# Instance normalisation in 3D: chunk sums split as two chunks on VectorE and one on ScalarE, and one mask of 27 entries that hands a matmul's result to chunks

## The chip, the cores and the metric

The kernel runs on one core of a Trainium2 chip; the other cores are idle. Times are device microseconds (us) of one execution. Every run is given a state, and only runs in the fast state are compared. HBM is the chip's main memory, SBUF a core's working memory, PSUM the memory that receives TensorE's results; DMA engines move data between HBM and SBUF, and a transfer that is issued can stand in a DMA queue: in the kernel before, a tile's store took 54.2 us from issue to landing, while one tile was stored every 29.0. A tile is a block of 128 partitions x 12288 fp32 values, 6.29 MB. A tile's *landing* is the moment at which its load from HBM is complete, and its *store issue* the moment at which its way back to HBM is ordered.

## The reference

```python
# x: float32 (8, 64, 32, 64, 64), eps: 1e-5
mean = np.mean(x, axis=(2, 3, 4), keepdims=True)
var = np.var(x, axis=(2, 3, 4), keepdims=True)
return (x - mean) / np.sqrt(var + eps)
```

There are 8 x 64 = 512 instances of 131072 values each, 268.4 MB in and 268.4 MB out.

## The kernel before

The tensor is read once and written once. It is cut into two small parts of 128 x 4096 and 42 tiles of 128 x 12288. Four tiles have a place in SBUF at a time, the four *slots*. SyncE issues the loads, ScalarE the stores; a slot is loaded again when its store is complete. One row of a tile holds three *chunks* of 4096, each from one instance; one instance lies in 32 consecutive chunks. So a mean needs three steps: sums of chunks, a sum over 32 chunks that lie on several partitions (a matmul with a block matrix of 1/n), and handing the result back to each chunk. The same is done for the squares.

```python
def over_instance(eng, a, p, at, m, to, negate, c1, wait, steps):   # runs on VectorE
    n = THIRDS                                                      # 3
    ...
    eng.tensor_tensor(out=block(a, by_both, n, m), in0=spread(a, at, m),
                      in1=belongs[:, :, :m], op=Alu.mult)._wait_ge(*wait).then_inc(steps[0], 1)
    # here TensorE multiplies by_both with the block matrix into psum p
    eng.tensor_reduce(out=a[:, by_instance : by_instance + n], in_=p..., axis=AXIS, op=Alu.add)
    eng.tensor_tensor(out=block(a, by_chunk, n, n), in0=spread(a, by_instance, n),
                      in1=belongs[:, :, :n].rearrange("p i c -> p c i"), op=Alu.mult)
    eng.tensor_reduce(out=a[:, to : to + n], in_=block(a, by_chunk, n, n), axis=AXIS,
                      op=Alu.add, negate=negate)                    # waits and increments cut

def tile_on_vector(eng, t, lane, c1, c3, c4, c16):
    ...
    for j, part in ((0, chunk[0]), (3, t[:, COLS - TURN :])):       # 4096, and 1536 of chunk 2
        eng.reduce_sum(out=column(a, SUMS, j), in_=part, axis=AXIS)._wait_ge(
            landed[lane], c16).then_inc(summed[lane], 1)
    over_instance(...)                                              # means
    ...  # chunk 0: subtract the mean, sum of squares
    over_instance(...)                                              # variances
    ...  # 1/root, shifts; chunk 0 and chunk 1 scaled in place

def tile_on_scalar(eng, t, lane, c1, c3, c4, c16, dst):
    ...
    for j, part in ((1, chunk[1]), (2, chunk[2][:, : CHUNK - TURN])):   # 4096, and 2560 of chunk 2
        eng.activation(out=unused..., in_=part, func=Act.Identity,
                       accum_out=column(a, SUMS, j))
    ...  # sums of squares of chunks 1 and 2, root, chunk 2 scaled in place
    eng.dma_start(out=dst, in_=t)._wait_ge(done[lane], c3).then_inc(stored[lane], 16)

def load_all(eng):                                                  # on SyncE
    ...
    with eng.Fori(1, ROUNDS) as it:
        for s in range(SLOTS):
            eng.dma_start(out=slots[s][:], in_=x_t[it * SLOTS + s])._wait_ge(
                stored[s], c16).then_inc(landed[s], 16)
```

The last tile has code of its own (`last_on_vector` and so on), which the change doesn't touch.

## Time and profile before

| | before |
|---|---|
| time, median of 6 runs | 1247.28 us (1247.02 to 1249.46) |
| moved over HBM | 536.9 MB, 431 GB/s over the span |
| busy: VectorE, ScalarE, TensorE | 65%, 61%, 4% |
| pace in the middle | one tile per 29.0 us |
| landing to store issue, a middle tile | 21.9 us |

The shares of the page are averages over the run, and none of them says by itself what sets the end. Two more readings are needed. The first is the page's list of DMA issues (kB each, median us from issue to landing):

```profile
slot<-in_x_dram SPq DMA_DIRECT2D x42, 6144.0 KB, 39.9
out_dram<-slot ACTq DMA_DIRECT2D x41, 6144.0 KB, 54.2
```

The second is one tile in the timeline (start, us, engine, line and operation; in brackets the idle time ahead of it):

```profile
653.89 6.08 DVE L173 TENSOR_REDUCE small<-slot 128x1 f32<-128x4096 f32 x2 [7.03 <-DMA slot<-in_x_dram]
...
660.00 0.17 DVE L141 TENSOR_TENSOR small<-small,belongs 128x12 f32<-128x12 f32 x1
660.23 0.50 PEld L266 LDWEIGHTS psum<-small,avg 128*128 128x128 f32 x2 [19.39 <-DVE small L141]
660.23 0.60 PE L266 MATMUL psum<-small,avg 128*128 128x12 f32 x2 [19.29 <-DVE small L141]
660.86 0.17 DVE L147 TENSOR_REDUCE small<-psum 128x3 f32<-128x12 f32 x1 [0.69 <-PE psum L266]
661.07 0.17 DVE L153 TENSOR_TENSOR small<-small,belongs 128x9 f32<-128x9 f32 x1
661.27 0.16 DVE L159 TENSOR_REDUCE small<-small 128x3 f32<-128x9 f32 x1
...
675.77 0.34 ACTq L256 DMA_DIRECT2D out_dram<-slot  x1
```

The first line is the tile's landing, the last its store issue. The three lines after the matmul (L147, L153, L159) are the hand-out that the change shortens: each starts 0.20 us after the one ahead of it.

### The profile page before, as it was taken

The numbers are of one execution on the slowest core, as the hardware profiler recorded it, in microseconds if no ns is written. First come the engines' busy times: TensorE is split into PE (matmuls) and PEld (weight loads), VectorE is DVE, ScalarE is ACT, GpSimd is POOL, SyncE is SP. The second block draws the span as 40 slices with busy tenths as digits, with TensorE's granted clock in tenths as the row PEclk, the third lists the DMA queues.
The fourth block names the chain that finished last, engine by engine and source line by source line (L and its number), as shares of the span: only waits on it lengthen the run. The fifth ranks groups of instructions, "written<-read, shape, count | busy, mean of one in ns | idle before, by whom it ended". The sixth has DMA issues, their size and how long they took to land.

```text
span 1245.3 us, 1977 instructions
## 1 busy us (share of the span) xinstructions
PE 52.7 (4%) x176; PEld 44.1 (4%) x176; DVE 808.7 (65%) x739; ACT 753.7 (61%) x435; POOL 4.0 (0%) x21
## 2 busy tenths in 40 slices
PE   0000000000000000000000000000000000000000
PEld 0000000000000000000000000000000000000000
DVE  2887666666666666666666666666666666666662
ACT  5876555666566666655556665666566555566661
POOL 1000000000000000000000000000000000000000
DMA  9999999999999999999999999999999999999998
GB/s 396 429 430 433 444 433 433 429 431 437 439 433 431 429 433 440 437 429 433 429 436 440 434 429 431 434 437 439 431 429 431 433 440 439 429 431 429 436 440 366
DMA packets 12818, 536.89 MB, mean 431 GB/s; under 512 B 1424, under 2 KB 1424, under 8 KB 1424
## 3 DMA queue, kind: packets, MB, share of 16 engines
q1 hardware_dynamic: 6336, 268.44, 49.9%
q10 hardware_dynamic: 6480, 268.44, 49.8%
q14 instruction: 2, 0.02, 0.0%
HBM read 268.44 MB, written 268.44 MB: 431 GB/s over the span
## 4 chain that ended last, share of the span: by engine, by line
another core or an unknown queue 82%; DMA 9%; DVE 3%; ACT 2%; SPq 1%; issue 1%; PE 0%; ACTq 0%; DVEq 0%
DMA slot<-in_x_dram 6%; DMA out_dram<-slot 4%; ACT unused L236 1%; SPq L543 1%; DVE stats L332 1%; DVE small L173 0%; ACT unused L229 0%; DVE slot L216 0%; DVE slot L209 0%; ACT slot L422 0%; PE psum L266 0%; DVE slot L372 0%; PE psum L435 0%; SPq L541 0%
## 5 line engine op out<-in xcount | busy, mean ns | idle before, releaser
L229 ACT ACTIVATE unused<-slot 128x4096 uint8<-128x4096 f32 x82 | 243.4, 2968 | 302.9 <-DMA slot<-in_x_dram 300.5
L173 DVE TENSOR_REDUCE small<-slot 128x1 f32<-128x4096 f32 x82 | 249.2, 3081 | 272.8 <-DMA slot<-in_x_dram 272.8
L236 ACT ACTIVATE unused<-slot,small 128x4096 uint8<-128x4096 f32 x82 | 303.4, 3701 | 63.7 <-DVE small L159 63.7
L187 DVE CUSTOM_DVE_ANT_0 unused<-slot 128x4096 uint8<-128x4096 f32 x41 | 181.4, 4426 | 1.4
L249 ACT ACTIVATE slot<-slot,small 128x4096 f32<-128x4096 f32 x41 | 155.9, 3801 | 18.0 <-DVE small L204 18.0
L216 DVE TENSOR_SCALAR slot<-slot,small 128x4096 f32<-128x4096 f32 x41 | 98.7, 2406 | 0.0
L180 DVE TENSOR_SCALAR slot<-slot,small 128x4096 f32<-128x4096 f32 x41 | 96.5, 2353 | 1.5
L266 PE MATMUL psum<-small,avg 128*128 128x9 f32 (+1 forms) x164 | 49.1, 375 | 1116.7 <-DVE small L141 1116.7
L209 DVE TENSOR_SCALAR slot<-slot,small 128x4096 f32<-128x4096 f32 x41 | 96.2, 2346 | 0.0
L266 PEld LDWEIGHTS psum<-small,avg 128*128 128x128 f32 x164 | 41.1, 311 | 1124.7 <-DVE small L141 1124.7
L147 DVE TENSOR_REDUCE small<-psum 128x3 f32<-128x12 f32 x82 | 13.8, 169 | 56.6 <-PE psum L266 56.6
L243 ACT ACTIVATE small<-small,eps_t 128x3 f32<-128x3 f32 x41 | 12.2, 299 | 61.1 <-DVE small L159 61.1
L141 DVE TENSOR_TENSOR small<-small,belongs 128x12 f32<-128x12 f32 x82 | 13.9, 169 | 31.2 <-ACT unused L236 28.8
L201 DVE RECIPROCAL small<-small 128x3 f32<-128x3 f32 x41 | 7.2, 175 | 15.0 <-ACT small L243 15.0
L153 DVE TENSOR_TENSOR small<-small,belongs 128x9 f32<-128x9 f32 x82 | 13.9, 170 | 2.8
L229 ACT ACTIVATION_READ_ACCUMULATOR unused<-slot 128x1 f32 x82 | 15.3, 187 | 0.0
L236 ACT ACTIVATION_READ_ACCUMULATOR unused<-slot,small 128x1 f32 x82 | 15.3, 187 | 0.0
L159 DVE TENSOR_REDUCE small<-small 128x3 f32<-128x9 f32 x82 | 13.3, 162 | 2.8
L332 DVE BATCH_NORM_STATS2 stats<-slot 128x6 f32<-128x512 f32 (+1 forms) x15 | 8.8, 662 | 7.2 <-DMA slot<-in_x_dram 7.2
L448 DVE TENSOR_REDUCE small<-slot 128x1 f32<-128x2048 f32 x2 | 4.6, 2282 | 8.9 <-DMA slot<-in_x_dram 8.9
L390 ACT ACTIVATE unused<-slot 128x4096 uint8<-128x4096 f32 (+1 forms) x2 | 4.4, 2208 | 8.0 <-DMA slot<-in_x_dram 8.0
L474 ACT ACTIVATE unused<-slot,small 128x4096 uint8<-128x4096 f32 x2 | 7.4, 3707 | 2.0 <-DVE small L451 2.0
(50 smaller groups left out, 52.4 us busy)
## 6 DMA issues: line engine op xcount, KB each, us to landing
slot<-in_x_dram SPq DMA_DIRECT2D x42, 6144.0 KB, 39.9
out_dram<-slot ACTq DMA_DIRECT2D x41, 6144.0 KB, 54.2
out_dram<-slot ACTq DMA_DIRECT2D x3, 2048.0 KB, 23.6
slot<-in_x_dram SPq DMA_DIRECT2D x2, 2048.0 KB, 10.0
out_dram<-slot ACTq DMA_DIRECT2D x1, 4096.0 KB, 17.6
```

The source lines that it names most:

```text
L141: eng.tensor_tensor(out=block(a, by_both, n, m), in0=spread(a, at, m), in1=belongs[:, :, :m], op=Alu.mult,)._wait_ge(*wait).then_inc(steps ...
L153: eng.tensor_tensor(out=block(a, by_chunk, n, n), in0=spread(a, by_instance, n), in1=belongs[:, :, :n].rearrange("p i c -> p c i"), op=Alu ...
L173: eng.reduce_sum(out=column(a, SUMS, j), in_=part, axis=AXIS)._wait_ge(landed[lane], c16).then_inc(summed[lane], 1)
L180: eng.tensor_scalar(out=chunk[0], in0=chunk[0], scalar1=column(a, MEANS, 0), scalar2=None, op0=Alu.add,)._wait_ge(centred[lane], c1).then_ ...
L187: eng.tensor_tensor_reduce(out=unused[2][:], in0=chunk[0], in1=chunk[0], scale=1.0, scalar=0.0, op0=Alu.mult, op1=Alu.add, accum_out=colum ...
L209: eng.tensor_scalar(out=chunk[0], in0=chunk[0], scalar1=column(a, SCALES, 0), scalar2=None, op0=Alu.mult,)._wait_ge(scaled[lane], c1).then ...
L216: eng.tensor_scalar(out=chunk[1], in0=chunk[1], scalar1=column(a, SCALES, 1), scalar2=column(a, SHIFTS, 1), op0=Alu.mult, op1=Alu.add,)._w ...
L229: eng.activation(out=unused[j - 1][:, : part.shape[1]], in_=part, func=Act.Identity, accum_out=column(a, SUMS, j),)._wait_ge(landed[lane], ...
L236: eng.activation(out=unused[j - 1][:], in_=chunk[j], func=Act.Square, bias=column(a, MEANS, j), accum_out=column(a, SQUARES, j),)._wait_ge ...
L249: eng.activation(out=chunk[2], in_=chunk[2], func=Act.Identity, scale=column(a, SCALES, 2), bias=column(a, SHIFTS, 2),)._wait_ge(shifted[l ...
L266: eng.matmul(out=p[:, col : col + THIRDS * m], lhsT=avg[PART][:], rhs=a[:, at + m : at + m + THIRDS * m], start=True, stop=True,)._wait_ge ...
L332: i = eng.bn_stats(out=stats[:, g, :], in_=t[:, at : at + size])
```

## The change

Its intent is to have fewer instructions: one reduction on VectorE covers chunks 0 and 1 and gives two columns at once, ScalarE sums chunk 2 whole, and after each matmul one multiplication with a mask of 3 x 9 entries and one reduction take the place of reduce, multiply, reduce.

```diff
-        for j, part in ((0, chunk[0]), (3, t[:, COLS - TURN :])):
-            eng.reduce_sum(out=column(a, SUMS, j), in_=part, axis=AXIS)...
+        eng.reduce_sum(
+            out=a[:, SUMS : SUMS + 2],
+            in_=t[:, : 2 * CHUNK].rearrange("p (c f) -> p c f", f=CHUNK),
+            axis=AXIS,
+        )._wait_ge(landed[lane], c16).then_inc(summed[lane], 1)
 ...
-        for j, part in ((1, chunk[1]), (2, chunk[2][:, : CHUNK - TURN])):
-            eng.activation(out=unused[j - 1]..., in_=part, func=Act.Identity, accum_out=column(a, SUMS, j))
+        eng.activation(out=unused[0][:], in_=chunk[2], func=Act.Identity, accum_out=column(a, SUMS, 2))
 ...
-        eng.tensor_reduce(out=a[:, by_instance : by_instance + n], in_=p..., axis=AXIS, op=Alu.add)
-        eng.tensor_tensor(out=block(a, by_chunk, n, n), in0=spread(a, by_instance, n), in1=belongs..., op=Alu.mult)
+        eng.tensor_tensor(
+            out=block(a, by_chunk, n, n * n),
+            in0=p.unsqueeze(1).to_broadcast([P, n, n * n]),
+            in1=belongs9[:].rearrange("p c i j -> p c (i j)"),
+            op=Alu.mult,
+        )
         eng.tensor_reduce(
             out=a[:, to : to + n],
-            in_=block(a, by_chunk, n, n),
+            in_=block(a, by_chunk, n, n * n),
```

The rest of the diff (cut) is the multiply and the matmul ahead of the hand-out, which shrink from 12 to 9 columns for the means, setup of the mask by three small copies on GpSimd, columns of the scratch tiles, and counts of semaphores.

More of the change, by code (lines that the diff above doesn't have):

```diff
@@ L68 @@
     within = sbuf("within", [P, PART * THIRDS, THIRDS])
-    TURN = 1536
-    belongs = sbuf("belongs", [P, THIRDS, THIRDS + 1])
+    belongs = sbuf("belongs", [P, THIRDS, THIRDS])
+    belongs9 = sbuf("belongs9", [P, THIRDS, THIRDS, THIRDS])
     GROUP = 480
@@ L87 @@
     late = sbuf("late", [P, 96])
-    small = [sbuf(f"small{i}", [P, 72]) for i in range(LANES)]
+    small = [sbuf(f"small{i}", [P, 96 if i < SLOTS else 16]) for i in range(LANES)]
     psum = [
@@ L109 @@
     sorted_ = semaphores("sorted", SLOTS)
-    joined = semaphores("joined", SLOTS)
     picked = semaphores("picked", SLOTS)
@@ L114 @@
     sorted2 = semaphores("sorted2", SLOTS)
-    joined2 = semaphores("joined2", SLOTS)
     picked2 = semaphores("picked2", SLOTS)
     gathered = semaphores("gathered", SLOTS)
-    SUMS, MEANS, SQUARES, VARS, ROOTS, SCALES, SHIFTS = 0, 28, 31, 55, 58, 61, 64
+    SUMS, MEANS, SQUARES, VARS, ROOTS, SCALES, SHIFTS = 0, 39, 42, 81, 84, 87, 90
     AXIS = mybir.AxisListType.X
@@ L129, in block, with over_instance @@
         return a[:, first : first + n * m].rearrange("p (n m) -> p n m", m=m)
-    def spread(a, first, m):
-        return a[:, first : first + m].unsqueeze(1).to_broadcast([P, THIRDS, m])
-    def over_instance(eng, a, p, at, m, to, negate, c1, wait, steps):
+    def over_instance(eng, a, p, at, to, negate, c1, wait, steps):
         n = THIRDS
-        by_both = at + m
-        by_instance = by_both + n * m
-        by_chunk = by_instance + n
+        by_both = at + n
+        by_chunk = by_both + n * n
         eng.tensor_tensor(
-            out=block(a, by_both, n, m),
-            in0=spread(a, at, m),
-            in1=belongs[:, :, :m],
+            out=block(a, by_both, n, n),
+            in0=a[:, at : at + n].unsqueeze(1).to_broadcast([P, n, n]),
+            in1=belongs[:],
             op=Alu.mult,
         )._wait_ge(*wait).then_inc(steps[0], 1)
-        eng.tensor_reduce(
-            out=a[:, by_instance : by_instance + n],
-            in_=p.rearrange("p (n m) -> p n m", m=m),
-            axis=AXIS,
-            op=Alu.add,
-        )._wait_ge(steps[1], c1).then_inc(steps[2], 1)
-        eng.tensor_tensor(
-            out=block(a, by_chunk, n, n),
-            in0=spread(a, by_instance, n),
-            in1=belongs[:, :, :n].rearrange("p i c -> p c i"),
-            op=Alu.mult,
-        )._wait_ge(steps[2], c1).then_inc(steps[3], 1)
+        eng.tensor_tensor(
[3 more added lines that the diff above has]
+            op=Alu.mult,
+        )._wait_ge(steps[1], c1).then_inc(steps[2], 1)
         eng.tensor_reduce(
             out=a[:, to : to + n],
-            in_=block(a, by_chunk, n, n),
+            in_=block(a, by_chunk, n, n * n),
             axis=AXIS,
@@ L164, in over_instance, with tile_on_vector @@
             negate=negate,
-        )._wait_ge(steps[3], c1).then_inc(steps[4], 1)
-    def tile_on_vector(eng, t, lane, c1, c3, c4, c16):
+        )._wait_ge(steps[2], c1).then_inc(steps[3], 1)
+    def tile_on_vector(eng, t, lane, c1, c2, c3, c16):
         a, p = small[lane], psum[lane]
         chunk = [t[:, i * CHUNK : (i + 1) * CHUNK] for i in range(THIRDS)]
-        for j, part in ((0, chunk[0]), (3, t[:, COLS - TURN :])):
-            eng.reduce_sum(out=column(a, SUMS, j), in_=part, axis=AXIS)._wait_ge(
-                landed[lane], c16
-            ).then_inc(summed[lane], 1)
+        eng.reduce_sum(
[3 more added lines that the diff above has]
+        )._wait_ge(landed[lane], c16).then_inc(summed[lane], 1)
         over_instance(
-            eng, a, p[:, 0:12], SUMS, 4, MEANS, True, c1, (summed[lane], c4),
-            (sorted_[lane], meaned[lane], joined[lane], picked[lane], centred[lane]),
+            eng, a, p[:, 0:9], SUMS, MEANS, True, c1, (summed[lane], c2),
+            (sorted_[lane], meaned[lane], picked[lane], centred[lane]),
         )
@@ L197, in tile_on_vector @@
         over_instance(
-            eng, a, p[:, 12:21], SQUARES, 3, VARS, False, c1, (squared[lane], c3),
-            (sorted2[lane], varied[lane], joined2[lane], picked2[lane], gathered[lane]),
+            eng, a, p[:, 9:18], SQUARES, VARS, False, c1, (squared[lane], c3),
+            (sorted2[lane], varied[lane], picked2[lane], gathered[lane]),
         )
@@ L223, in tile_on_vector, with tile_on_scalar @@
         )._wait_ge(shifted[lane], c1).then_inc(done[lane], 1)
-    def tile_on_scalar(eng, t, lane, c1, c3, c4, c16, dst):
+    def tile_on_scalar(eng, t, lane, c1, c2, c3, c16, dst):
         a = small[lane]
         chunk = [t[:, i * CHUNK : (i + 1) * CHUNK] for i in range(THIRDS)]
-        for j, part in ((1, chunk[1]), (2, chunk[2][:, : CHUNK - TURN])):
-            eng.activation(
-                out=unused[j - 1][:, : part.shape[1]],
-                in_=part,
-                func=Act.Identity,
-                accum_out=column(a, SUMS, j),
-            )._wait_ge(landed[lane], c16).then_inc(summed[lane], 1)
+        eng.activation(
+            out=unused[0][:],
+            in_=chunk[2],
+            func=Act.Identity,
+            accum_out=column(a, SUMS, 2),
+        )._wait_ge(landed[lane], c16).then_inc(summed[lane], 1)
         for j in (1, 2):
@@ L258, in tile_on_scalar, with tile_on_tensor @@
         )
-    def tile_on_tensor(eng, t, lane, c1, c3, c4, c16):
+    def tile_on_tensor(eng, t, lane, c1, c2, c3, c16):
         a, p = small[lane], psum[lane]
-        for at, m, col, before, after in (
-            (SUMS, 4, 0, sorted_, meaned),
-            (SQUARES, 3, 12, sorted2, varied),
+        n = THIRDS
+        for at, col, before, after in (
+            (SUMS, 0, sorted_, meaned),
+            (SQUARES, n * n, sorted2, varied),
         ):
             eng.matmul(
-                out=p[:, col : col + THIRDS * m],
+                out=p[:, col : col + n * n],
                 lhsT=avg[PART][:],
-                rhs=a[:, at + m : at + m + THIRDS * m],
+                rhs=a[:, at + n : at + n + n * n],
                 start=True,
@@ L278, with last_on_vector @@
     BOTH2, INST2, CHUNKED2, FOUND, ROOTED, SCALED, SHIFTED = 53, 65, 68, 77, 80, 83, 86
-    def last_on_vector(eng, t, lane, c1, c3, c4, c16):
+    def last_on_vector(eng, t, lane, c1, c2, c3, c16):
         a, p = late, psum[lane]
@@ L383, with last_on_scalar @@
     WEIGHED, WEIGHED2, VARIED, STEPS = 4, 11, 14, 16
-    def last_on_scalar(eng, t, lane, c1, c3, c4, c16, dst):
+    def last_on_scalar(eng, t, lane, c1, c2, c3, c16, dst):
         a = late
@@ L431, in last_on_scalar, with last_on_tensor @@
         ).then_inc(stored[lane], 16)
-    def last_on_tensor(eng, t, lane, c1, c3, c4, c16):
+    def last_on_tensor(eng, t, lane, c1, c2, c3, c16):
         for col, at, ready_at in ((0, BOTH, WEIGHED), (12, BOTH2, WEIGHED2)):
@@ L514, in over_tiles @@
             ctx.enter_context(eng.register(f"{on_tile.__name__}_c{m}"))
-            for m in (1, 3, 4, 16)
+            for m in (1, 2, 3, 16)
         ]
-        for c, m in zip(counts, (1, 3, 4, 16)):
+        for c, m in zip(counts, (1, 2, 3, 16)):
             eng.reg_mov(c, m)
@@ L522, in over_tiles @@
                 on_tile(eng, slots[s][:], s, *counts, *more)
-            for c, m in zip(counts, (1, 3, 4, 16)):
+            for c, m in zip(counts, (1, 2, 3, 16)):
                 eng.reg_add(c, c, m)
@@ L528, in over_tiles @@
             step = on_last if k == n_tiles - 1 else on_tile
-            step(eng, slots[k % SLOTS][:], k % SLOTS, c, 3 * c, 4 * c, 16 * c, *more)
+            step(eng, slots[k % SLOTS][:], k % SLOTS, c, 2 * c, 3 * c, 16 * c, *more)
     def load_all(eng):
@@ L603, in set_up @@
                 eng.tensor_tensor(
-                    out=belongs[:, :, :THIRDS],
-                    in0=within[:, 0:THIRDS, :] if b == 1 else belongs[:, :, :THIRDS],
+                    out=belongs[:],
+                    in0=within[:, 0:THIRDS, :] if b == 1 else belongs[:],
                     in1=within[:, b * THIRDS : (b + 1) * THIRDS, :],
@@ L609, in set_up @@
             )
-        step(
-            eng.tensor_copy(
-                out=belongs[:, :, THIRDS:], in_=belongs[:, :, THIRDS - 1 : THIRDS]
+        for j in range(THIRDS):
+            step(
+                eng.tensor_copy(
+                    out=belongs9[:, :, :, j], in_=belongs[:].rearrange("p i c -> p c i")
+                )
             )
-        )
         for to, c in ((slice(0, THIRDS), slice(0, THIRDS)), (slice(3, 4), slice(1, 2))):
```

## The prediction

> **What bounds the kernel now.** I read the page first (shares of the engines, the DMA row of the 40 slices, the queues), then the windows of one stretch in the middle, then the DMA queues in that same stretch, then who waits for whom. From the page:
>
> ```profile
> PE 52.7 (4%) x176; PEld 44.1 (4%) x176; DVE 808.7 (65%) x739; ACT 753.7 (61%) x435; POOL 4.0 (0%) x21
> DMA  9999999999999999999999999999999999999998
> q1 hardware_dynamic: 6336, 268.44, 49.9%
> q10 hardware_dynamic: 6480, 268.44, 49.8%
> HBM read 268.44 MB, written 268.44 MB: 431 GB/s over the span
> ```
>
> No compute engine is above two thirds, while the DMA row is at its highest digit in every slice but the last. Loads (q1) and stores (q10) each take half of the 16 engines, 99.7% together. The input is read once and the output written once, so the bytes can't shrink. The steady state, four tiles long, in the windows view (columns: stretch, length, busy time of each engine, granted clock, DMA share, GB/s) and then the two queues in that stretch (packets, MB, share):
>
> ```profile
> 600.00:716.00 116.00, 4.79 (x16) 4.00 (x16) 76.52 (x69) 70.49 (x41) 0.00 (x0) 1.00 1.00 434
> ...
> q10 hardware_dynamic: 576, 25.17, 50.1%
> q1 hardware_dynamic: 576, 25.17, 50.1%
> ```
>
> The DMA share is 1.00 and both queues get the same 25.17 MB, four tiles each, in 116.0 us: one tile in and one out per 29.0 us. VectorE works 76.52/4 = 19.1 us of each 29.0, ScalarE 17.6. The waits say the same from the engines' side (engine and line waited for: total us, times, longest):
>
> ```profile
> ACT unused L229 <- DMA slot<-in_x_dram: 300.5, 39, 8.2
> DVE small L173 <- DMA slot<-in_x_dram: 272.8, 39, 7.5
> ...
> SPq L543 <- DMA out_dram<-slot: 1024.5, 36, 28.7
> ```
>
> Both engines wait some 7 to 8 us per tile for a load, and the loading queue waits 28.5 us per tile for a store to free a slot. The last row alone could also be read as a latency loop round the four slots; that is the first rival below.
>
> [...] 434 GB/s at a share of 1.00. So there is nothing to win in the steady state. [...] 576 packets from each queue in the stretch above. So a store that is issued later stands behind what is queued and loses no bandwidth, as long as something is queued. [...] the step from 1536 to 4096 elements costs (4420 - 1742)/2560 = 1.046 ns per element, 0.956 elements per ns. So the reduction over two chunks should gain no speed from its shape.
>
> **The change, part by part.** The rows are those of the groups by form (count, busy us, mean ns):
>
> ```profile
> L173 DVE TENSOR_REDUCE small<-slot 128x1 f32<-128x4096 f32 x41 | 181.2, 4420 | 272.8 <-DMA slot<-in_x_dram 272.8
> L229 ACT ACTIVATE unused<-slot 128x2560 uint8<-128x2560 f32 x41 | 95.1, 2320 | 0.0
> L173 DVE TENSOR_REDUCE small<-slot 128x1 f32<-128x1536 f32 x41 | 71.4, 1742 | 0.0
> L153 DVE TENSOR_TENSOR small<-small,belongs 128x9 f32<-128x9 f32 x82 | 13.9, 170 | 2.8
> L159 DVE TENSOR_REDUCE small<-small 128x3 f32<-128x9 f32 x82 | 13.3, 162 | 2.8
> L147 DVE TENSOR_REDUCE small<-psum 128x3 f32<-128x12 f32 x41 | 7.0, 170 | 28.4 <-PE psum L266 28.4
> ```
>
> (1) The sums on VectorE. Before, 4096 and 1536 elements in two instructions, which the timeline shows as 6.08 us together (they overlap a little, 4420 + 1742 = 6162 ns). After, 8192 elements in one: 4420 + 4096 x 1.046 = 8.70 us. That is +2.62 us on the path from a tile's landing to its store, because the means need it.
> (2) The sums on ScalarE. Before 3617 + 2320 ns plus two reads of an accumulator, done about when VectorE is; after one of 3617 ns plus one read, about 3.8 us. This frees 2.4 us of ScalarE per tile, but takes nothing from the path: VectorE's 8.70 us now end last.
> (3) The hand-out after each of the two matmuls. Before: reduce, multiply, reduce, each starting 0.20 us after the one ahead. After: one multiply over 27 and one reduce over 27. A step is gone (0.20 us); the two that remain have 18 elements more, and I take about 1 ns each from the slope of (1), so +0.02 us each. Saved per hand-out 0.16 us, per tile 0.33 us. That one input of the multiply is in PSUM should not matter: the reduce from PSUM takes 170 ns, as the step of the same kind in SBUF does.
> (4) The multiply ahead of the first matmul has 9 elements instead of 12, and the matmul 9 columns instead of 12: 3 ns and 6 ns by their rows, nothing. The setup on GpSimd gets two more tiny copies, 0.2 us each, while the first load is still on its way (it lands at 8.9 us, setup ended near 6).
>
> Sum per tile: 2.62 - 0.33 = **+2.3 us** from landing to store. A middle tile lands at 653.89 us and its store is issued at 675.77: 21.9 us before, so 24.2 after. VectorE's busy time goes from 19.1 to 19.1 + 8.70 - 6.16 - 0.34 + 0.08 = 21.4 us of 29.0, ScalarE's from 17.6 to about 15.1.
>
> Now what of it reaches the end. In a slot's round, a load takes 39.9 us from issue to landing, the work 21.9 and a store 54.2: 116.0, four times 29.0. But a load and a store need only 29.0 us each at their half of the bandwidth, so 39.9 + 54.2 - 58.0 = 36.1 us per round is standing in a queue. The added 2.3 us comes out of these 36.1, and the pace stays at 29.0. At the start, tile 0 is stored at 52.7 us and the next two follow at 22.2 us, the pace of the engines; they would come at 24.5 us, so the third is stored at 104 instead of 97.2. But then the store queue is still on tile 1's store, which lands at 120.4, so no DMA engine runs dry. At the end, the last tile has its own code, which the change leaves alone (16.4 us from its landing at 1205.96 to its first store at 1222.35). From 1222 us on, 7.57 MB move, of which the last tile is 6.29: 1.28 MB, 3 us of work, is still queued when that store is issued. The store of the tile before goes out 2.3 us later, at 1201, still well inside that queue. So the sum on the time is 0, give or take a microsecond.
>
> **The rivals.** (a) **A latency loop.** If the four slots' round were the bound, each round would grow by 2.3 us, each tile by 2.3/4 = 0.58 us, and 41 tiles by 24 us: 1271 us, 1.9% slower. For it speaks the loading queue's wait of 1024.5 us for stores; against it that the DMA share is 1.00 and 434 GB/s during that wait, which leaves no room. (b) **VectorE becomes the bound.** It would need over 29.0 us per tile; I reckon 21.4. Only if the two-row reduction ran at half speed (8.7 us more) would a tile take 33 us from landing to store; the next tile's sums follow on the same engine, so 41 tiles would need some 1350 us. Nothing in the trace points to it. (c) **The shorter hand-out wins.** 0.33 us per tile off the path, were the path the bound and the sums equal: 3 us at most. It meets the same full DMA. (d) **Start or end.** If the last store found an empty queue because the load of the last tile landed later, some 1 to 3 us are lost; if the later stores let the loads run ahead and the tail stays fuller (its share is 0.89 in 1222 to 1227), about 0.5 us is won.
>
> **Range and chances.** I take the time before, 1247.4 us, unchanged. The three runs before spread from 1247.1 to 1249.5, and (d) adds at most 3 us, so 1244 to 1252 should hold it eight times in ten. Faster by over 2% [...]: 0.01. Slower by over 2% needs a reduction far slower than its slope, or (a) with somewhat more than I reckon: 0.02. Within 2%: 0.97.
>
> **What would show it.** In the profile after: the two-chunk reduction near 8.7 us; the reduce from PSUM gone and a multiply from PSUM of about 0.19 us in its place; landing to store near 24.2 us; VectorE's wait for loads down from 272.8/39 = 7.0 to about 4.7 us per tile, ScalarE's up; load and store latency together shorter by about 2.3 us; stores still spaced by 29.0 us, at 434 GB/s. I would be wrong if the pace were 29.6 us with a DMA share under 1.00 (then (a) holds), if VectorE no longer waited for loads (then (b)), or if the DMA moved fewer GB/s at a full share, for which I have no mechanism.

Four passages are cut from the prediction, at the marks, because no trace or run shows what they said. No term of its sum is among them: +2.3 us per tile is 2.62 - 0.33, from the rows that it quotes, and the sum on the time is 0. Some of its steps rest on less with the cuts. That there is nothing to win in the steady state, and the 0.01 for faster by over 2%, rest on the 434 GB/s at a share of 1.00 alone. That a later store loses no bandwidth was the author's estimate at that time; the runs after it showed it (434 GB/s before and after the change). That the reduction gains no speed from its shape rests on the measured slope of 1.046 ns per element alone.

## The result, and the profile after

| | before | after |
|---|---|---|
| time, median of 6 runs each | 1247.28 us | 1246.41 us (1246.21 to 1248.0) |
| ratio | | 0.9991 (95% interval 0.9978 to 1.0004) |
| VectorE, ScalarE busy | 808.7, 753.7 us | 904.6, 658.6 us |
| load, work, store of a slot's round | 39.9 + 21.9 + 54.2 us | 39.9 + 24.2 + 51.9 us |
| pace | 29.0 us | 29.0 us |

A ratio here is the mean time of one kernel's fast runs over the mean of the other's from the same rounds, so it is not quite the ratio of the medians. The interval contains 1: the time is the same. VectorE took on 95.9 us of work and ScalarE gave up 95.1, and neither can be seen in the time.

First the shares, the DMA row and the DMA issues of the page after, then the window and waits that answer to those of the prediction:

```profile
PE 52.5 (4%) x176; PEld 44.1 (4%) x176; DVE 904.6 (73%) x616; ACT 658.6 (53%) x353; POOL 4.4 (0%) x23
DMA  9999999999999999999999999999999999999998
...
slot<-in_x_dram SPq DMA_DIRECT2D x42, 6144.0 KB, 39.9
out_dram<-slot ACTq DMA_DIRECT2D x41, 6144.0 KB, 51.9
```

```profile
600.00:716.00 116.00, 4.77 (x16) 4.00 (x16) 85.88 (x57) 61.21 (x32) 0.00 (x0) 1.00 1.00 434
```

```profile
ACT unused L224 <- DVE small L147: 256.9, 41, 6.3
ACT unused L217 <- DMA slot<-in_x_dram: 209.5, 38, 6.1
DVE small L160 <- DMA slot<-in_x_dram: 182.6, 38, 5.4
```

The stretch of four tiles again has a DMA share of 1.00 at 434 GB/s; only the busy times of VectorE (85.88/4 = 21.5 us per tile) and ScalarE (15.3, with 15.1 predicted) have moved. A store takes 2.3 us less from issue to landing, which is just what the work takes more. One tile in the timeline after, the last that the changed code handles:

```profile
1176.21 8.69 DVE L160 TENSOR_REDUCE small<-slot 128x2 f32<-128x8192 f32 x1 [4.91 <-DMA slot<-in_x_dram]
...
1185.80 0.18 DVE L141 TENSOR_TENSOR small<-psum,belongs 128x27 f32<-128x27 f32 x1 [0.69 <-PE psum L255]
1186.02 0.18 DVE L147 TENSOR_REDUCE small<-small 128x3 f32<-128x27 f32 x1
...
1200.37 0.35 ACTq L244 DMA_DIRECT2D out_dram<-slot  x1
```

From 1176.21 to 1200.37 is 24.16 us from landing to store issue, and the tile that lands at 654.17 takes as long. VectorE's wait ahead of the tile has shrunk from 7.03 to 4.91 us: the longer work came out of that wait and out of the store's time in the queue.

### The profile page after: what moved, and what is told of

The parts are those of the page before. It is cut to its first block, busy times and chain, and to the rows that moved or that the text cites. A ratio compares the mean times of both kernels' runs of the same rounds, so it can differ in the third digit from the quotient of the medians.

```text
span 1244.6 us, 1774 instructions
## 1 busy us (share of the span) xinstructions
PE 52.5 (4%) x176; PEld 44.1 (4%) x176; DVE 904.6 (73%) x616; ACT 658.6 (53%) x353; POOL 4.4 (0%) x23
## 4 chain that ended last, share of the span: by engine, by line
another core or an unknown queue 80%; DMA 9%; DVE 5%; ACT 2%; SPq 1%; issue 1%; PE 0%; ACTq 0%; DVEq 0%
DMA slot<-in_x_dram 6%; DMA out_dram<-slot 4%; DVE small L160 2%; ACT unused L224 2%; SPq L532 1%; DVE stats L321 1%; DVE slot L205 1%; DVE slot L198 1%; ACT slot L411 0%; PE psum L255 0%; DVE slot L361 0%; PE psum L424 0%; DVE small L141 0%; DVE small L147 0%
## 5 line engine op out<-in xcount | busy, mean ns | idle before, releaser
L160 DVE TENSOR_REDUCE small<-slot 128x2 f32<-128x8192 f32 x41 | 356.1, 8686 | 182.6 <-DMA slot<-in_x_dram 182.6
L224 ACT ACTIVATE unused<-slot,small 128x4096 uint8<-128x4096 f32 x82 | 303.4, 3700 | 256.9 <-DVE small L147 256.9
L217 ACT ACTIVATE unused<-slot 128x4096 uint8<-128x4096 f32 x41 | 148.3, 3617 | 213.0 <-DMA slot<-in_x_dram 209.5
L255 PE MATMUL psum<-small,avg 128*128 128x9 f32 x164 | 48.9, 372 | 1118.8 <-DVE small L135 1118.8
L141 DVE TENSOR_TENSOR small<-psum,belongs 128x27 f32<-128x27 f32 x82 | 15.3, 187 | 56.4 <-PE psum L255 56.4
L147 DVE TENSOR_REDUCE small<-small 128x3 f32<-128x27 f32 x82 | 14.8, 181 | 2.8
L224 ACT ACTIVATION_READ_ACCUMULATOR unused<-slot,small 128x1 f32 x82 | 15.2, 186 | 0.0
L193 DVE TENSOR_TENSOR small<-small 128x3 f32<-128x3 f32 x41 | 6.7, 164 | 1.4
L217 ACT ACTIVATION_READ_ACCUMULATOR unused<-slot 128x1 f32 x41 | 7.6, 186 | 0.0
L460 ACT ACTIVATE unused<-slot 128x2048 uint8<-128x2048 f32 x2 | 3.8, 1910 | 6.9 <-DMA slot<-in_x_dram 6.5
## 6 DMA issues: line engine op xcount, KB each, us to landing
slot<-in_x_dram SPq DMA_DIRECT2D x42, 6144.0 KB, 39.9
out_dram<-slot ACTq DMA_DIRECT2D x41, 6144.0 KB, 51.9
```

The source lines that it names most:

```text
L141: eng.tensor_tensor(out=block(a, by_chunk, n, n * n), in0=p.unsqueeze(1).to_broadcast([P, n, n * n]), in1=belongs9[:].rearrange("p c i j - ...
L160: eng.reduce_sum(out=a[:, SUMS : SUMS + 2], in_=t[:, : 2 * CHUNK].rearrange("p (c f) -> p c f", f=CHUNK), axis=AXIS,)._wait_ge(landed[lane ...
L217: eng.activation(out=unused[0][:], in_=chunk[2], func=Act.Identity, accum_out=column(a, SUMS, 2),)._wait_ge(landed[lane], c16).then_inc(su ...
L224: eng.activation(out=unused[j - 1][:], in_=chunk[j], func=Act.Square, bias=column(a, MEANS, j), accum_out=column(a, SQUARES, j),)._wait_ge ...
L255: eng.matmul(out=p[:, col : col + n * n], lhsT=avg[PART][:], rhs=a[:, at + n : at + n + n * n], start=True, stop=True,)._wait_ge(before[la ...
```

## The experiments

The theory: the DMA engines are full from start to end, loads and stores stand in queues, and any change to the work between landing and store is taken out of the time in queues, as long as the engines keep up with 29.0 us per tile. The main rival: the round of a slot is a loop of fixed latencies, so added work counts a quarter each. The other: the hand-out's saving is on the path, and the sums' cost isn't. All kernels gave results that passed the comparison with the reference (a weak test on this input, as the copy below shows); runs of one table ran on the same chip beside the kernel before.

**One part at a time.** The kernel before with only the new sums, and with only the new hand-out:

```diff
 # e1_sums_only, from before          # the hand-out keeps its four steps, with 3 columns
-        for j, part in ((0, chunk[0]), (3, t[:, COLS - TURN :])):
+        eng.reduce_sum(out=a[:, SUMS : SUMS + 2], in_=t[:, : 2 * CHUNK].rearrange(...), axis=AXIS)
 # e2_handout_only, from before       # the sums keep their split; masks of 36 and 27 entries
-        reduce, multiply by belongs, reduce
+        multiply by masks[m] (3 x 3 x m), reduce
```

> The kernel before with only the sums changed (one VectorE instruction over two chunks, one on ScalarE; the hand-out keeps its four steps). DMA-bound theory: landing to store about 21.9 + 2.6 = 24.5 us, store latency shorter by the same 2.6 us, pace still 29.0 us per tile at 434 GB/s, time 1246 to 1248 us. Latency-loop rival (the round of a slot is the bound): 2.6/4 us per tile more, some 27 us: 1274 us.

> The kernel before with only the hand-out changed (one mask instead of three steps; the sums keep their split, so the first mask has 36 entries, the second 27). DMA-bound theory: landing to store about 21.6 us, 0.3 less than before, store latency longer by the same 0.3 us, time 1246 to 1248 us. Rival that the shorter hand-out is what the time follows: 3 us less at most, 1244 us.

| | time, median | ratio to before (95%) | landing to store | load, store latency |
|---|---|---|---|---|
| before, same rounds | 1247.12 | | 21.88 | 39.9, 54.2 |
| sums only | 1247.77 | 1.0009 (0.9993 to 1.0026) | 24.50 | 39.9, 51.6 |
| hand-out only | 1246.92 | 0.9999 (0.9983 to 1.0016) | 21.57 | 39.9, 54.5 |

The landing and store lines of one middle tile, sums only first, then hand-out only:

```profile
654.18 8.69 DVE L172 TENSOR_REDUCE small<-slot 128x2 f32<-128x8192 f32 x1 [4.55 <-DMA slot<-in_x_dram]
678.68 0.34 ACTq L257 DMA_DIRECT2D out_dram<-slot  x1
```

```profile
653.92 6.08 DVE L163 TENSOR_REDUCE small<-slot 128x1 f32<-128x4096 f32 x2 [7.46 <-DMA slot<-in_x_dram]
675.49 0.34 ACTq L246 DMA_DIRECT2D out_dram<-slot  x1
```

The sums cost 24.50 - 21.88 = 2.62 us of path and the hand-out saves 0.31; together 2.31 against the 2.28 measured for the whole change. Each store's latency moved by as much the other way, and neither time moved. The latency loop's 1274 us for the first is refuted. For the second, the rival's 1244 was too near to 1247 for the time alone to refute it well, but the store's latency of 54.5 shows where the 0.3 us went.

**More work, until it shows.** The kernel after with an additional reduction on VectorE ahead of the sums, its result unused, over 4096 and over 8192 elements:

```diff
+        eng.reduce_sum(out=a[:, 93:94], in_=t[:, :CHUNK], axis=AXIS)._wait_ge(landed[lane], c16)   # e3; e4: 93:95, 2 * CHUNK
         eng.reduce_sum(
             out=a[:, SUMS : SUMS + 2],
```

> The kernel after with one more reduction of 4096 elements (4.4 us) on VectorE ahead of the sums, its result unused. DMA-bound theory: landing to store about 28.6 us, VectorE about 25.8 us of 29.0 busy, its wait for loads nearly gone, store latency down to about 47.5 us, pace still 29.0, time 1245 to 1248 us. Latency-loop rival: 4.4/4 us per tile more, 45 us: about 1292 us.

> The kernel after with one more reduction of 8192 elements (8.7 us) on VectorE ahead of the sums, its result unused. DMA-bound theory: landing to store becomes about 32.9 us, and since tiles follow each other on the engines the pace becomes about 32.7 us instead of 29.0, so the engines' chain is the bound: about 1247 + 41 x 3.7 = 1390 to 1400 us, VectorE no longer waiting for loads, DMA share about 0.89. Latency-loop rival: 8.7/4 us per tile more, about 1336 us.

| | time, median | ratio to before (95%) | first reduction to store issue, a middle tile | pace |
|---|---|---|---|---|
| + 4096 elements | 1246.95 | 0.9998 (0.9982 to 1.0015) | 28.5 | 29.0 |
| + 8192 elements | 1403.73 | 1.1254 (1.1235 to 1.1273) | 32.75 | 32.63 |

The windows of the same stretch, with 4096 more and then with 8192 more, and of the latter the shares of the chain that ended last:

```profile
600.00:716.00 116.00, 4.78 (x16) 4.01 (x16) 104.27 (x61) 63.12 (x33) 0.00 (x0) 1.00 1.00 434
```

```profile
600.00:716.00 116.00, 4.77 (x16) 4.00 (x16) 105.39 (x59) 57.26 (x30) 0.00 (x0) 1.00 0.93 381
```

```profile
DVE 68%; ACT 23%; PE 4%; issue 2%; DMA 2%; SPq 0%; DVEq 0%; ACTq 0%
```

With 4.4 us more, VectorE is 90% busy in that stretch and still the time is the same at 434 GB/s. With 8.7 us more the DMA share falls to 0.93 (0.89 expected) and the rate to 381 GB/s, the chain that ended last runs over VectorE and ScalarE instead of the DMA, and stores are issued every 32.63 us. So there is no slope, as a latency loop would have (1292 and 1336 us), but a threshold: 28.5 us of work per tile cost nothing and 32.75 us did, and the theory puts it at 29.0 between them. The work that counts is the whole chain from landing to store, since one tile's chain hardly overlaps the next one's: VectorE is 91% busy in the second of the two stretches, and the pace is that of the chain. The change took some 2.2 of the 7.0 us that lay between; the kernel after has some 5 us left. My figure for the last run was low by a few us (1390 to 1400), and the traces show why. In this run 41 tiles follow each other at 32.63 us, from 31.79 us to the start of the last tile's work at 1369.40, and 33.5 us come after. In the kernel before, the same 41 steps run from 30.84 to 1205.96, 28.66 us each and not 29.0, mainly because the first tiles went at the engines' pace of 22.2; 39.3 us come after. So 41 x 3.7 = 152 us should have been 162.5 plus 1.0 at the start, less 5.8 at the end. The median store latency with 4096 more was 45.0 and not 47.5 us: in part of the run tiles had landed before VectorE was free (it waited for a load 19 times only), and that time is part of the round too.

**No work at all.** The kernel after with all arithmetic removed: each store waits only for its load. Its output is its input, wrong (that the comparison passes it says only that the random input is nearly of mean 0 and variance 1 already; so a pass tells little of the other kernels' means and variances either).

```diff
-    over_tiles(nc.vector, ...); over_tiles(nc.tensor, ...); over_tiles(nc.scalar, part_on_scalar, tile_on_scalar, ...)
+    def copy_tile(eng, t, lane, c1, c2, c3, c16, dst):
+        eng.dma_start(out=dst, in_=t)._wait_ge(landed[lane], c16).then_inc(stored[lane], 16)
+    over_tiles(nc.scalar, copy_part, copy_tile, copy_last, with_target=True)
```

> The kernel after without any arithmetic: the same loads and stores in the same slots, each store waiting only for its load (the output is the input, wrong on purpose). DMA-bound theory: the time is what the transfers alone need, 536.9 MB at about 434 GB/s and a few us of start and end, so 1238 to 1246 us, at most 10 us under the kernels. If the engines' work or the slots' round set the time, the copy would be far faster: latency-loop rival, 24.2/4 us per tile less, about 1000 us.

It took 1247.35 us (1246.81 to 1249.38), ratio to before 0.9994 (0.9978 to 1.0011). From its page:

```profile
DMA  9999999999999999999999999999999999999998
...
slot<-in_x_dram SPq DMA_DIRECT2D x42, 6144.0 KB, 64.8
out_dram<-slot ACTq DMA_DIRECT2D x41, 6144.0 KB, 51.0
```

Load and store now take 64.8 + 51.0 = 115.8 us: the round is as long as ever with no work in it. The 24 us of the arithmetic are replaced by time in the queues. I had allowed up to 10 us for the work of the last tile; not even that is in the time, which lies 1 us above the range that I gave. So this kernel, before as after, costs what its transfers cost, and with this traffic even the removal of all arithmetic did not make it faster.

**Fewer slots.** With fewer slots there is less standing in queues (load plus store latency was 65.1 us with three, against 94.1 with four), so this takes away what hides the work:

```diff
-    SLOTS = 4
+    SLOTS = 3          # and 2
-    ROUNDS = n_tiles // SLOTS
+    ROUNDS = (n_tiles - 1) // SLOTS
```

> The kernel before with three slots instead of four (and the last tile kept out of the loop). DMA-bound theory: a round is 21.9 us of work and at least 29 us each for load and store at half the bandwidth, 79.9 us, under the 87.0 of three tiles at 29.0, so the pace stays close to 29.0 and the time within some 10 us of 1247; load plus store latency falls from 94.1 to about 65 us. Latency-loop rival (latencies are what they are): (39.9 + 21.9 + 54.2)/3 = 38.7 us per tile, about 1640 us.

> The kernel after with three slots. DMA-bound theory: 24.2 + 58 = 82.2 us per round, still under 87.0, so the same time as the kernel before with three slots within 5 us; the slack of queues is down to about 5 us, so a small loss may show here. Latency-loop rival: 2.3/3 us per tile more than the kernel before with three slots, some 31 us.

> The kernel before with two slots. DMA-bound theory: the queues can no longer be kept full: 21.9 us of work and a store and a load of 14.5 us at the full rate [...] make 55 us at best against 58.0 for two tiles, and more wherever the two slots' transfers overlap, so between 1250 and 1450 us with a DMA share under 1. Latency-loop rival: 116/2 = 58 us per tile, about 2400 us.

One term is cut from this expectation, a guess that no trace stood behind when it was made. What is left of the sum, 21.9 + 14.5 + 14.5, comes to 50.9 us; with the cut term it came to 55.

> The kernel after with two slots. DMA-bound theory: with no standing queue left, the 2.3 us more of work per tile can show for the first time: up to 2.3/2 us per tile, 47 us, slower than the kernel before with two slots, and at least not faster. If it isn't slower at all, the longer work is hidden by something else than the standing queue.

| | before | after | ratio of each to the unchanged kernel |
|---|---|---|---|
| 3 slots, median us of fast runs | 1270.60 | 1278.06 | 1.0183 (unclear at 2%), 1.0244 |
| 2 slots, median us of fast runs | 1425.95 | 1440.65 | 1.1428, 1.1534 |

One of the four runs of the kernel after with three slots (1299.92 us) was over 1.5% above the fastest; it is not in the ratio, and the median of the other three is 1278.06. The windows of the kernel after with two slots show where the queues run dry:

```profile
655.00:682.00 27.00, 1.33 (x5) 1.04 (x5) 21.94 (x17) 15.41 (x9) 0.00 (x0) 1.00 0.99 417
682.00:685.00 3.00, 0.00 (x0) 0.00 (x0) 2.97 (x2) 3.00 (x1) 0.00 (x0) 1.00 1.02 442
685.00:688.00 3.00, 0.00 (x0) 0.00 (x0) 3.00 (x1) 3.00 (x3) 0.00 (x0) 1.00 0.00 0
```

For 3 us the DMA moved nothing at all while VectorE and ScalarE were busy throughout. Over a longer stretch, two slots before and then after:

```profile
600.00:1000.00 400.00, 14.39 (x48) 12.04 (x48) 234.85 (x207) 216.53 (x124) 0.00 (x0) 1.00 0.94 384
600.00:1000.00 400.00, 14.32 (x48) 12.03 (x48) 257.66 (x169) 183.69 (x97) 0.00 (x0) 1.00 0.92 377
```

With two slots before, the shortest load took 17.3 us and the shortest store 15.9, against an estimate of 14.5 each from 6.29 MB at 434 GB/s. With two slots the change costs time: 14.7 us between the medians, 0.36 us per tile, well above the spread of either (at most 4.2 us). That is the sign that I expected, and less than my upper limit of 47 us. With three slots the loss is 7.5 us between the medians of fast runs that spread over about 9 us in each kernel, more than the 5 us expected; the sign agrees, the size I would not rely on. I missed the level with three slots: I had allowed 10 us over 1247 and it was 23. Load and store latency did fall to 32.7 + 32.4 = 65.1 us, as expected, 7.1 us above two times 29.0, so the queues are nearly empty. The window of the kernel before with three slots shows what the loss looks like:

```profile
600.00:716.00 116.00, 4.80 (x16) 4.01 (x16) 73.40 (x68) 67.34 (x39) 0.00 (x0) 1.00 1.01 427
```

The DMA share is full, but fewer GB/s move. From 40 to 1200 us, at a mean share of 1.00, it is 428 GB/s against 434 with four slots; that is 16 of the 18 us by which the profiled run (1265.07 us) is longer. This is the sign for which the prediction had no mechanism (fewer GB/s at a full share), and why the packets take longer stays open. It also means that a DMA share of 1.00 alone does not prove that nothing is lost: read the GB/s beside it. Fixed latencies are refuted by these runs (1640 and 2400 us): the latencies shrink with the number of slots, as time in a queue does.

## Why the prediction was right

- **What bounds the kernel.** The DMA, said the prediction from a share of 1.00 at 434 GB/s. The copy without arithmetic, at 0.9994 of the time before, shows that the transfers set the time (434 GB/s in the copy too, from 120 to 1166 us); which part of their path is the limit (DMA engines, ports or HBM) no run here separates. One reading was weaker than the prediction said: 576 packets from each queue follow from four loads and four stores in the stretch, and show nothing of the order in which the queues were served (from 62 to 72 us they are 52 and 38). What the argument needed, that a later store loses no bandwidth, is shown by the unchanged 434 GB/s.
- **Costs of the parts.** The two-chunk reduction: 8.70 us predicted, 8.69 measured, so its shape gave no speed and took none. The multiply from PSUM 0.19 predicted, 0.187 measured; the last reduction 0.18. ("The step of the same kind in SBUF" was a multiply set beside a reduction; the true pair before, reductions of 9 elements, took 167 ns from PSUM and 162 in SBUF, so the step stands.) The hand-out 0.33 predicted, 0.31 measured alone. Landing to store: 24.2 predicted, 24.16 measured. VectorE 21.4 us per tile predicted, 21.5 measured.
- **Where the cost went.** Out of the 36.1 us of a round that stand in queues (an estimate, 39.9 + 54.2 less two times 29.0): load and store latency together fell from 94.1 to 91.8 us. All of it came from the store.
- **The start.** The third store was predicted at 104 us and came at 102.82. The term mis-sized is "at 24.5 us" for the pace of the engines: it is 24.03. I added 2.3 to 22.2, but in the 22.2 ScalarE had been the last to finish its sums (VectorE's next step waited 0.51 us for it), and that wait went with the change. It hid behind the store queue all the same.
- **The waits.** VectorE's for loads fell from 7.0 to 182.6/38 = 4.8 us per tile (4.7 predicted). ScalarE's for loads was predicted to rise, and that was wrong: it fell from 300.5 to 209.5 us. ScalarE's freed time appears a step later, as the wait for the means (L224 waiting for L147), up from 63.7 to 256.9 us.
- **The rivals.** The latency loop's 1271 us is refuted by the result, though still within 2% of the time before, so a verdict at 2% alone could not have told the two apart; the sums alone, both additions, the copy and fewer slots refute it too, and only the hand-out alone could not. The engines as the bound are real: with the 8192 elements the chain took 32.75 us per tile, more than 29.0, and the pace was 32.63. The 1350 us given for that case (8.7 us more) was too low: it is about 41 x 33, which leaves out the start and the end, and the run took 1403.73. Of the end, the kernel after was 0.87 us faster in the median, and its last tile landed 0.73 us earlier in the trace; but the sums alone and the hand-out alone landed it 0.4 us earlier too and their times don't differ from before, so I don't count it as an effect of the change.

## What to carry to other kernels

Where the transfers set the time and enough buffers are in flight, ask of a change to the arithmetic only whether a tile's work (here the whole chain from landing to store) stays under the pace of the transfers: in these runs 28.5 us of work were free under a pace of 29.0, and with 32.75 us the pace was 32.63. Load, work and store of a buffer added up to the four buffers times 29.0 us with 21.9 us of work, with 24.2 and with none (load plus store 94.1, 91.8 and 115.8 us), so a shorter stage merely lengthened the stay in a queue. A wait for a DMA is not by itself a sign of latency (the loading queue waited 1024.5 us for stores while the DMA moved 434 GB/s): look at the DMA share and the GB/s during the wait. To find out what all the arithmetic is worth, run the transfers alone; and keep the buffers that make the queues, since with two slots the same change cost 14.7 us.
